# A decoder layer on one core: the same instructions put in order by another of the scheduler's estimates

## The chip, the core and the metric

The kernel runs on one core of one Trainium2 chip. A core has a matrix engine (TensorE, PE in the rows below, with its weight loads as PEld), three elementwise engines (VectorE or DVE, ScalarE or ACT, GpSimd or POOL), an engine that here only issues transfers (SyncE, SP), 16 DMA engines, and two on-chip memories, SBUF for operands and PSUM for the sums of the matmuls. Each engine works off its own list of instructions and waits for the others through semaphores. The metric is the device time of one execution in microseconds, here of one core.

## What is computed

One layer of a decoder for 256 tokens of width 2048, in float32. The reference, cut to its steps:

```python
mod = silu(c) @ w_ada + b_ada                        # shift, scale, gate for both halves
sh1, sc1, g1, sh2, sc2, g2 = split(mod, 6)
h = rmsnorm(x, norm1_g) * (1 + sc1) + sh1
proj = h @ w_in                                      # 2048 x 4928
hq, hf, hi, hg, q_a, kv_a, k_pe = split(proj)
o_a = rmsnorm(hgrn2_chunked(hq, hf, hi, lb)) * silu(hg)         # 8 heads, chunks of 64
qh = rmsnorm(q_a) @ w_q_up ; kv = rmsnorm(kv_a) @ w_kv_up       # latent attention, 8 heads
o_b = rmsnorm(causal_attention(qh, kh, v))                      # blocks of 128 queries
x = x + g1 * (concat(o_a, o_b) @ w_out)
h2 = rmsnorm(x, norm2_g) * (1 + sc2) + sh2
x = x + g2 * moe(h2)        # best of 4 groups, best 2 of its 8 experts, 32 experts in all
```

All weights are read from memory once, 572 MB, of which 403 MB are the 32 experts' matrices.

## The kernel before

The weights come as a stream of chunks, most of them 2 MB (128 partitions by 4096), in a fixed list `items`. `ring_fill` (L163) issues the loads on SP as slots come free: four slots in the first part, two more from the output projection on (L830), one more before the experts (L868). `ring_done` (L181) returns a slot. The list is consumed in order by a loop that calls one function for each kind of chunk.

The first part holds everything ahead of the experts. `ad1_chunk` (L243) and `adt_chunk` (L264) make the shift and scale of the first norm; the first takes its chunks through TensorE (L252), the second, for twelve chunks that lie transposed in memory, through VectorE with two passes over 2048 columns each (L271, results named `adt`), which are given the scheduler's `high_priority(-120)`. `ada_chunk` (L283) makes g1, sh2, sc2 and g2 out of eight chunks each, with eight matmuls per chunk onto one row (L293, `pada`); its end for g1 and g2 is four additions on one partition (L302). `dense` (L410) is every projection: each 512-column tile of the weights is split into a high and a low part by ScalarE (L417) and VectorE (L418), both written to a tile named `split` of which there are four, and six matmuls (L425 to L427 or L432 to L434, accumulator `pacc`) use it. The input projection's partial sums are added in SBUF by VectorE (L457, `proj`). `mla` (L707) is the latent attention of four heads, called twice: scores `psc` (L786, L788), mask, maximum and exponential (L791 to L797), transposes `ppT` (L802) and their copy `pT` (L804), the product with v `pov` (L810), division (L814, `o`), norm over each head (L477 to L479, L195 to L202), multiplication (L818) and transposes `pmt` (L824). `hgrn` (L483) is the recurrence of four heads, also called twice: gates (L490 to L498, with a sigmoid L491 and a logarithm L497 on ScalarE), scan (L501), exponentials and products (L503 to L515), transposes `ptr` (L520), `pA`, `ua`, `ub`, `uc`, `po`. Then follow the output projection with the residual (`w_out`) and the router.

In the second part, 32 experts of six chunks each pass by: gate and up matmuls (L1040, `pgu`), down matmuls (L1016, `py`), gathering the tokens (L970) and adding the outputs (L993).

What stands where in the lists of the engines is decided when the program is built. The framework (`tile.TileContext`) takes the instructions as the code emits them, keeps the dependencies between tiles, and orders them by priority and by an estimate of when each can start. In the kernel before the estimate is a simple one. The list of loads, SPREAD, EARLY and the buffer counts are written by hand and are the same in both.

## Time and profile before

| | us |
|---|---|
| median of 3 runs | 1505.64 (1505.19 to 1507.08) |
| profiled execution | 1505.27 |
| its span | 1503.0 |
| TensorE busy | 1127.9 (75%) |
| VectorE busy | 588.6 (39%) |
| ScalarE busy | 338.4 (23%) |
| mean transfer rate | 383 GB/s |

The span is the time from the first to the last event of the profile; the execution's own time has 2.3 us around it. The shares are means over two parts that differ, so the page is read by slices and windows first, then by what each engine waited for in a window. A busy TensorE is not one at its peak: its matmuls overlap, so where a count matters the distance from one matmul's start to the next is used.

### The profile page before, as it was taken

The numbers are of one execution on the slowest core, as the hardware profiler recorded it, in microseconds if no ns is written. First come the engines' busy times: TensorE is split into PE (matmuls) and PEld (weight loads), VectorE is DVE, ScalarE is ACT, GpSimd is POOL, SyncE is SP. The second block draws the span as 40 slices with busy tenths as digits, with TensorE's granted clock in tenths as the row PEclk, the third lists the DMA queues.
The fourth block names the chain that finished last, engine by engine and source line by source line (L and its number), as shares of the span: only waits on it lengthen the run. The fifth ranks groups of instructions, "written<-read, shape, count | busy, mean of one in ns | idle before, by whom it ended". The sixth has DMA issues, their size and how long they took to land.

```text
span 1503.0 us, 22846 instructions
## 1 busy us (share of the span) xinstructions
PE 1127.9 (75%) x9893; PEld 687.8 (46%) x9893; DVE 588.6 (39%) x1200; ACT 338.4 (23%) x699; POOL 5.0 (0%) x9
## 2 busy tenths in 40 slices
PE   5989999979999989675666666657657756666556
PEld 2868887737568756333323323323423423332222
DVE  4699998769765552220120121113112112112112
ACT  5634446536435423000100100100100100000000
POOL 0000000000000000000000000000000000000000
PEclk7999999989999999888888888879888889779787
DMA  9788796877979798999999999999999999999995
GB/s 373 263 332 356 298 352 257 315 302 313 369 293 376 293 373 343 430 429 430 430 430 430 430 430 429 429 431 430 430 430 430 430 431 430 430 429 429 431 430 222
DMA packets 44143, 575.61 MB, mean 383 GB/s; under 512 B 4858, under 2 KB 5114, under 8 KB 8712
## 3 DMA queue, kind: packets, MB, share of 16 engines
q1 hardware_dynamic: 42496, 570.56, 91.4%
q10 hardware_dynamic: 1544, 3.56, 0.6%
q8 instruction: 79, 1.29, 0.3%
q14 instruction: 24, 0.20, 0.0%
HBM read 572.00 MB, written 2.11 MB: 382 GB/s over the span
## 4 chain that ended last, share of the span: by engine, by line
DMA 51%; PE 37%; DVE 9%; ACT 1%; issue 1%; SPq 0%; ACTq 0%; DVEq 0%
DMA wch<-in_w_gu_dram 37%; DMA wch<-in_w_down_dram 13%; PE pgu L1040 5%; PE pacc L433 5%; PE pacc L434 5%; PE pacc L432 5%; PE pada L293 3%; PE py L1016 3%; PE pcmb L993 2%; PE pgat L970 2%; DVE wch L271 2%; DVE split L418 2%; DVE proj L457 1%; PE pacc L427 1%; PE pacc L425 1%; PE pacc L426 1%
## 5 line engine op out<-in xcount | busy, mean ns | idle before, releaser
L1040 PE MATMUL pgu<-wch,XT 128*32 128x256 f32 x4096 | 309.7, 455 | 201.0 <-DMA wch<-in_w_gu_dram 201.0
L1040 PEld LDWEIGHTS pgu<-wch,XT 128*32 128x32 f32 x4096 | 139.2, 126 | 361.0 <-DMA wch<-in_w_gu_dram 253.9
L1016 PE MATMUL py<-wch,hT 128*32 128x256 f32 x2048 | 167.9, 485 | 76.8 <-DMA wch<-in_w_down_dram 72.1
L1020 DVE TENSOR_TENSOR Y<-py,gate 32x256 f32<-32x256 f32 x256 | 107.6, 420 | 216.5 <-PE py L1016 213.6
L1005 DVE TENSOR_TENSOR hid<-sgu,pgu 128x128 f32<-128x128 f32 x32 | 9.2, 287 | 462.2 <-ACT sgu L1003 462.2
L418 DVE TENSOR_TENSOR split<-wch,split 128x512 fp32r<-128x512 f32 (+2 forms) x248 | 159.5, 666 | 69.6 <-ACT split L417 69.0
L417 ACT ACTIVATE split<-wch 128x512 fp32r<-128x512 f32 (+2 forms) x248 | 148.0, 614 | 161.2 <-PE pacc L434 98.4
L1016 PEld LDWEIGHTS py<-wch,hT 128*32 128x32 f32 x2048 | 78.9, 133 | 155.0 <-issue 60.8
L1003 ACT ACTIVATE sgu<-pgu 128x128 f32<-128x128 f32 x32 | 8.9, 277 | 602.5 <-PE pgu L1040 602.5
L975 ACT ACTIVATE XT<-pgat,sh,a 128x128 f32<-128x128 f32 x128 | 48.1, 456 | 223.1 <-PE pgat L970 223.0
L433 PE MATMUL pacc<-split,hhi 128*128 128x512 f32 (+1 forms) x192 | 75.5, 393 | 7.0 <-DVE split L418 7.0
L425 PE MATMUL pacc<-hhi,split 128*128 128x256 f32 x256 | 72.4, 286 | 2.8 <-ACT hhi L388 2.2
L426 PE MATMUL pacc<-hlo,split 128*128 128x256 f32 x256 | 72.7, 285 | 1.7 <-DVE hlo L389 1.7
L434 PE MATMUL pacc<-split,hlo 128*128 128x512 f32 (+1 forms) x192 | 73.7, 386 | 0.0
L432 PE MATMUL pacc<-split,hhi 128*128 128x512 f32 (+1 forms) x192 | 72.9, 392 | 0.8 <-DVE proj L457 0.7
L427 PE MATMUL pacc<-hhi,split 128*128 128x256 f32 x256 | 72.2, 285 | 1.1 <-DVE split L418 1.1
L293 PE MATMUL pada<-wch,ca 128*1 128x512 f32 x512 | 68.7, 602 | 3.3 <-DVE pada L288 3.3
L993 PE MATMUL pcmb<-Y,pwt 128*128 128x512 f32 x128 | 59.2, 605 | 15.5 <-DVE Y L1020 15.5
L970 PEld LDWEIGHTS pgat<-ohr,x 128*128 128x128 f32 x512 | 63.4, 205 | 10.7 <-issue 9.8
L970 PE MATMUL pgat<-ohr,x 128*128 128x128 f32 x512 | 66.8, 291 | 0.7 <-DVE sm L937 0.7
L271 DVE SCALAR_TENSOR_TENSOR wch<-wch,gate 128x2048 f32<-128x2048 f32 x24 | 54.8, 2284 | 0.0
L457 DVE TENSOR_TENSOR proj<-proj,pacc 128x512 f32<-128x512 f32 (+1 forms) x80 | 51.2, 662 | 0.8 <-PE pacc L434 0.4
(311 smaller groups left out, 1215.4 us busy)
## 6 DMA issues: line engine op xcount, KB each, us to landing
wch<-in_w_gu_dram SPq DMA_DIRECT2D x128, 2048.0 KB, 31.1
wch<-in_w_down_dram SPq DMA_DIRECT2D x64, 2048.0 KB, 31.5
wch<-in_w_ada_dram SPq DMA_DIRECT2D x36, 2048.0 KB, 10.1
wch<-in_w_ada_t_dram SPq DMA_DIRECT2D x12, 2048.0 KB, 7.9
wch<-in_w_in_dram SPq DMA_DIRECT2D x12, 2048.0 KB, 9.2
wch<-in_w_out_dram SPq DMA_DIRECT2D x8, 2048.0 KB, 9.5
wch<-in_w_in_h_dram SPq DMA_DIRECT2D x8, 1024.0 KB, 8.9
wch<-in_w_in_dram SPq DMA_DIRECT2D x3, 1664.0 KB, 7.0
```

Source lines behind the costliest of these rows:

```text
L293: PE.matmul(acc[b][32 * j:32 * j + 1, :], ca[:, kt:kt + 1], w[:, o:o + 512], start=kt == 0, stop=kt == 15)
L417: S.activation(s[:, 0, :ncol], w, AF.Copy)
L418: V.tensor_sub(s[:, 1, :ncol], w, s[:, 0, :ncol])
L426: PE.matmul(o, s[:, 0, c], lo, start=False, stop=False, skip_group_check=True)
L432: PE.matmul(o, hi[:, c], s[:, 0, :ncol], start=first, stop=False)
L433: PE.matmul(o, hi[:, c], s[:, 1, :ncol], start=False, stop=False)
L434: PE.matmul(o, lo[:, c], s[:, 0, :ncol], start=False, stop=stop)
L970: PE.matmul(ps[:, 128 * i:128 * i + 128], x2[kt // 4][:, t, 128 * (kt % 4):128 * (kt % 4) + 128], ohr[:, t], start=t == 0, stop=t == 1)
L993: PE.matmul(ps, PWT[G4][:, 128 * t:128 * t + 128], Y4[j // 2][:, 512 * (j % 2):512 * (j % 2) + 512], start=True, stop=True)
L1016: PE.matmul(py[32 * j:32 * j + 32, :256], H["T"][:, 32 * kt:32 * kt + 32], w[:, 1024 * kt + 256 * j:1024 * kt + 256 * j + 256], start=kt = ...
L1020: V.tensor_mul(Y[q][r:r + 32, 256 * j:256 * j + 256], py[32 * j:32 * j + 32, :256], gate[32 * j:32 * j + 32, c:c + 256])
L1040: PE.matmul(gu[32 * j:32 * j + 32, :256], XT[G4][kt // 8][:, kt % 8, 32 * e4:32 * e4 + 32], w[:, 1024 * i + 256 * j:1024 * i + 256 * j + 2 ...
```

## The change

```diff
-    with tile.TileContext(nc) as tc:
+    with tile.TileContext(nc, schedule_with_timeline_sim=True) as tc:
```

The scheduler now orders the instructions by a simulation of the engines' timelines. The instructions and their tiles are the same, but for one table load more on ScalarE. In the lists of the engines 2,276 lines of TensorE differ, 943 of VectorE, 481 of ScalarE and 48 of SP, none of GpSimd.

SP at the start of the program (`x` the four pieces of the input, `cst` the constants, `wch` a chunk of weights), before and now in one piece:

```order
 L93 DMA pos_i<-in_pos_dram 128x2
-L172 DMA wch_97<-in_w_ada_dram 128x4096
 L212 DMA x_89<-in_x_dram 128x2x512
 L212 DMA x_90<-in_x_dram 128x2x512
 L212 DMA x_91<-in_x_dram 128x2x512
 L212 DMA x_92<-in_x_dram 128x2x512
+L172 DMA wch_97<-in_w_ada_dram 128x4096
 L217 DMA cst<-in_cst_dram 128x1120
 L172 DMA wch_102<-in_w_ada_dram 128x4096
```

The first chunk of weights has moved behind the four pieces of x.

VectorE at one of the transposed chunks (`wch_258`) in the second quarter of the input projection, before:

```order
L271 SCALAR_TENSOR_TENSOR wch_258_1585,adt_291_1822<-wch_258_1585,gate_84 128x2048
L457 TENSOR_TENSOR proj_66_383<-proj_66_383,pacc_278_1716 128x512
L457 TENSOR_TENSOR proj_66_383<-proj_66_383,pacc_279_1717 128x512
L418 TENSOR_TENSOR split_288_1800<-wch_256_1580,split_288_1800 128x512
L418 TENSOR_TENSOR split_289_1809<-wch_256_1580,split_289_1809 128x512
L280 TENSOR_TENSOR a1_132<-adt_291_1822,pc_79 128x1
L418 TENSOR_TENSOR split_295_1832<-wch_271_1694,split_295_1832 128x512
L281 SCALAR_TENSOR_TENSOR a1_132<-a1_132,pc_79 128x1
L418 TENSOR_TENSOR split_296_1841<-wch_271_1694,split_296_1841 128x512
L418 TENSOR_TENSOR split_297_1850<-wch_271_1694,split_297_1850 128x512
L457 TENSOR_TENSOR proj_71_406<-proj_71_406,pacc_284_1780 128x512
L457 TENSOR_TENSOR proj_71_406<-proj_71_406,pacc_285_1781 128x512
```

and now:

```order
L418 TENSOR_TENSOR split_261_1592<-wch_228_1379,split_261_1592 128x512
L418 TENSOR_TENSOR split_262_1601<-wch_228_1379,split_262_1601 128x512
L418 TENSOR_TENSOR split_263_1610<-wch_228_1379,split_263_1610 128x512
L457 TENSOR_TENSOR proj_47_274<-proj_47_274,pacc_250_1540 128x512
L457 TENSOR_TENSOR proj_47_274<-proj_47_274,pacc_251_1541 128x512
L271 SCALAR_TENSOR_TENSOR wch_258_1585,adt_291_1822<-wch_258_1585,gate_84 128x2048 x2
L418 TENSOR_TENSOR split_264_1619<-wch_228_1379,split_264_1619 128x512
L418 TENSOR_TENSOR split_267_1632<-wch_228_1379,split_267_1632 128x512
L418 TENSOR_TENSOR split_268_1647<-wch_228_1379,split_268_1647 128x512
L277 TENSOR_TENSOR sh1_131<-adt_291_1822,pc_79 128x1
L418 TENSOR_TENSOR split_269_1662<-wch_228_1379,split_269_1662 128x512
L280 TENSOR_TENSOR a1_132<-adt_291_1822,pc_79 128x1
```

The chunk's two passes, which had thirteen instructions between them, are now one behind the other (x2), and stand eleven splits earlier.

TensorE at the end of the second call of `mla`, before, where the last product `pov` lies 47 rows ahead of `pmt`:

```order
L427 MATMUL pacc_622_3604<-hhi_274_1704,split_626_3650 128x256
L293 MATMUL pada_612_3541<-wch_609_3530,ca_109 1x512 x8
L293 MATMUL pada_612_3541<-wch_613_3551,ca_109 1x512 x5
L824 MATMUL pmt_592_3382<-cst_78,o_565_3272 128x128 x4
L824 MATMUL pmt_593_3389<-cst_78,o_565_3272 128x128 x4
L312 MATMUL pcol_610_3533<-cst_78,rows_130 128x128 x4
```

and now:

```order
L788 MATMUL psc_579_3332<-kpT_558_3231,qz_363_2208 128x128
L802 MATMUL ppT_582_3348<-cst_78,s_580_3341 128x128 x4
L810 MATMUL pov_578_3327<-v_519_3051,pT_583_3353 128x128 x4
L824 MATMUL pmt_592_3382<-cst_78,o_565_3272 128x128 x4
L824 MATMUL pmt_593_3389<-cst_78,o_565_3272 128x128 x4
L312 MATMUL pcol_610_3533<-cst_78,rows_130 128x128 x4
L432 MATMUL pacc_664_3864<-split_670_3902,mhi_590_3380 128x512
```

The tiles of the input projection and the modulation chunks that stood between the scores, the product and `pmt` now stand ahead of the scores.

VectorE at the same place, before, from the division of the last product on:

```order
L814 TENSOR_TENSOR o_565_3272<-pov_578_3327,den_566_3273 128x512
L478 TENSOR_REDUCE sm_584_3362<-sq_585_3363 128x4
L418 TENSOR_TENSOR split_625_3635<-wch_608_3520,split_625_3635 128x512
L418 TENSOR_TENSOR split_626_3650<-wch_608_3520,split_626_3650 128x512
L515 TENSOR_TENSOR proj_71_406<-proj_71_406,sg_629_3671 128x1024
L478 TENSOR_REDUCE sm_584_3362<-sq_586_3366 128x4
L498 TENSOR_SCALAR proj_66_383<-proj_66_383 128x1024
L479 TENSOR_SCALAR sm_584_3362<-sm_584_3362 128x8
```

and now, from the copy ahead of it:

```order
L804 COPY pT_583_3353<-ppT_582_3348 128x512
L515 TENSOR_TENSOR proj_71_406<-proj_71_406,sg_629_3671 128x1024
L498 TENSOR_SCALAR proj_66_383<-proj_66_383 128x1024
L501 SCALAR_TENSOR_TENSOR b_630_3679<-cst_78,d1_631_3680 128x256
L814 TENSOR_TENSOR o_565_3272<-pov_578_3327,den_566_3273 128x512
L501 SCALAR_TENSOR_TENSOR b_630_3679<-cst_78,d1_631_3680 128x256 x3
L478 TENSOR_REDUCE sm_584_3362<-sq_585_3363 128x4
L478 TENSOR_REDUCE sm_584_3362<-sq_586_3366 128x4
L503 TENSOR_TENSOR d1_631_3680<-b_630_3679 128x1024
L504 TENSOR_TENSOR d3_632_3681<-b_630_3679 128x1024
L479 TENSOR_SCALAR sm_584_3362<-sm_584_3362 128x8
L511 TENSOR_TENSOR kn_633_3682<-kn_633_3682,proj_66_383 128x1024
```

The recurrence's scan, exponentials and products (L501 to L513) now stand ahead of the attention's norm, L818 is the seventh instruction behind the last row shown, and ScalarE has the sigmoid and the logarithm of the recurrence (L491, L497) and its four exponentials (L505 to L508) ahead of or among the steps of that norm.

## Rows read from the trace of the kernel before

**Rows 1.** Page, busy tenths of 40 slices of the span (9 is 90% or more).

```profile
PE   5989999979999989675666666657657756666556
...
DVE  4699998769765552220120121113112112112112
...
DMA  9788796877979798999999999999999999999995
```

**Rows 2.** Page, chain that ended last, shares of the span by engine.

```profile
DMA 51%; PE 37%; DVE 9%; ACT 1%; issue 1%; SPq 0%; ACTq 0%; DVEq 0%
```

**Rows 3.** Windows: stretch, length, busy us (instructions) by engine, PEclk, DMA share, GB/s.

```profile
0.00:60.00 60.00, 44.25 (x225) 27.26 (x226) 27.50 (x80) 34.93 (x64) 1.16 (x5) 0.86 0.82 314
60.00:214.00 154.00, 143.56 (x873) 123.08 (x872) 148.03 (x238) 69.50 (x121) 0.00 (x0) 0.99 0.86 330
...
354.00:432.00 78.00, 71.72 (x515) 47.51 (x513) 59.37 (x125) 37.34 (x69) 2.86 (x3) 0.98 0.77 307
...
573.00:1476.00 903.00, 589.74 (x6663) 297.93 (x6655) 162.86 (x370) 63.60 (x184) 0.00 (x0) 0.85 1.00 429
```

**Rows 4.** Timeline of PE, 469 to 473 us: start, us, engine, line, operation.

```profile
469.38 0.40 PE L432 MATMUL pacc<-split,mhi 128*128 128x512 f32 x1
...
470.78 0.40 PE L432 MATMUL pacc<-split,mhi 128*128 128x512 f32 x1
```

**Rows 5.** Waits of PE, 0 to 60 us: total, times, longest.

```profile
PE pad L252 <- DMA wch<-in_w_ada_dram: 9.9, 2, 9.6
```

**Rows 6.** Waits of SP, 0 to 60 us.

```profile
SPq L217 <- DMA wch<-in_w_ada_dram: 4.9, 1, 4.9
```

**Rows 7.** Timeline of DVE, 136 to 152 us (x4: four in a row).

```profile
136.08 2.28 DVE L271 SCALAR_TENSOR_TENSOR wch<-wch,gate 128x2048 f32<-128x2048 f32 x1
...
145.09 2.49 DVE L418 TENSOR_TENSOR split<-wch,split 128x512 fp32r<-128x512 f32 x4
```

**Rows 8.** DMA issues, 153.5 to 154.5 us: KB each, median us to landing.

```profile
wch<-in_w_ada_t_dram SPq DMA_DIRECT2D x1, 2048.0 KB, 7.8
```

**Rows 9.** Waits of PE, 214 to 241 us.

```profile
PE pqa L667 <- DVE proj L663: 2.5, 1, 2.5
```

**Rows 10.** Waits of PE, 241 to 340 us.

```profile
PE pmt L824 <- DVE o L818: 4.6, 1, 4.6
PE pada L293 <- DVE pada L288: 3.3, 1, 3.3
```

**Rows 11.** Line 302 in 300 to 312 us: duration ns min/median/max, first and last start.

```profile
L302 DVE TENSOR_TENSOR brows<-brows,pada x4: 667/682/694, 305.9 to 310.3; 1x512 f32<-1x512 f32 x4
```

**Rows 12.** Timeline of PE, 271 to 281 us.

```profile
272.53 0.39 PE L788 MATMUL psc<-kpT,qz 128*128 128x128 f32 x2
...
277.24 0.44 PE L802 MATMUL ppT<-cst,s 128*128 128x128 f32 x2
```

**Rows 13.** Timeline of ACT, 387 to 400 us.

```profile
394.45 1.28 ACT L491 ACT_TABLE_LOAD   x1
395.74 1.06 ACT L491 ACTIVATE sg<-proj 128x1024 f32<-128x1024 f32 x1
...
397.86 1.28 ACT L189 ACT_TABLE_LOAD   x1
```

**Rows 14.** Waits of PE, 340 to 461 us.

```profile
PE ptr L520 <- DVE d L513: 5.1, 1, 5.1
```

**Rows 15.** Groups of DVE by line, 390 to 425 us: busy us, mean ns of one.

```profile
L501 DVE TENSOR_TENSOR_SCAN b<-cst,d 128x256 f32<-128x256 f32 x4 | 2.7, 681 | 0.0
...
L503 DVE TENSOR_TENSOR d<-b 128x1024 f32<-128x1024 f32 x1 | 1.2, 1224 | 0.0
...
L818 DVE TENSOR_TENSOR o<-o,sm 128x1024 f32<-128x1024 f32 x1 | 1.2, 1197 | 0.0
```

**Rows 16.** Timeline of DVE, 565 to 568 us.

```profile
566.45 0.14 DVE L940 CAST rounds<-sm 1x1 int32<-1x1 f32 x1
```

**Rows 17.** Timeline of SP, 570 to 600 us.

```profile
573.41 8.02 SPq L172 DMA_DIRECT2D wch<-in_w_gu_dram  x3
```

## The prediction

> **What bounds the kernel now.** I read the view by slices first. From the 17th slice on (601 us) the transfers fill every slice and TensorE is half to three quarters busy [rows 1]; the chain that ended last is DMA for half of the span [rows 2]. The windows say the same: 573 to 1476 has a DMA share of 1.00 at 429 GB/s, while before 573 the share is 0.77 to 0.86 and TensorE or VectorE is full [rows 3]. So the program is two parts put end to end. The expert stream needs its 903 us whatever the order of the engines, as long as seven chunks lie ready when it starts; its order of instructions hardly moves. Only the first part, up to the first expert chunk consumed at 573 us, can gain or lose, and what it gains or loses goes one to one into the total. I therefore sum the shift of that point. The profiled execution took 1505.27 us (span 1503.0, 2.3 outside), 0.4 under the median of 1505.64, so the sum is made against 1505.3.
>
> In the first part the work is the same before and after: the same matmuls, the same elementwise instructions. What counts is how long TensorE stands. One 512-column tile of a projection occupies it for 1.40 us from first matmul to first matmul [rows 4]. All its matmuls up to 573 us, counted so, add up to about 477 us (matmul start to matmul start, over the timeline); about 78 us of the first 560 it stands, of which 22 in the first 60 us and some 17 in 60 to 214, where VectorE has 148 of 154 us busy and sets the pace [rows 3]. I go through the places where it stands, and ask what stands there in the new order.
>
> **Start: -4 us.** The first matmuls with a weight wait 9.9 us for two chunks of the shift and scale weights [rows 5]. In front of the second sits the load of the constants, which SP held back 4.9 us for the landing of the first chunk [rows 6]: in the built program the two share a completion counter. In the new order x goes out first and the constants share a counter with a small load, so the constants and all weight loads behind them leave up to 4.9 us earlier. x, 2 MB, now lands ahead of the first chunk, which needs it to wait but little: that part can't be worth more than 4.9, and I take 4 (2 to 6).
>
> **The VectorE stretch, 60 to 214 us: +8 us.** Here each of the eleven later transposed chunks costs VectorE two passes of 2.28 us, 2.21 each when the next instruction is at hand [rows 7]. Before, they stand apart, with four to ten split and add instructions between them; VectorE makes a split in 0.60 us [rows 7] and TensorE uses it up in 1.40, so one pass of 2.21 is covered by the three or four splits that lie ready. Now both stand together, 4.42 us. I follow two cycles. VectorE makes three splits, does two adds on a finished accumulator and goes into the pair; the splits behind wait for its end. TensorE has used up its stock and stands 4.0 us in the first cycle; in the next the adds themselves must wait 1.5 us for matmuls that were held up, the pair ends later, and TensorE stands 2.2 us; in a third it is 2.8. Eleven times the mean of 3.0 is 33 us, against 17 before: +16. VectorE's own total up to the end of this stretch is 1 us smaller than before, so by its work alone nothing is lost but the waits for loads below: +4. Worked forward from the last pair but one (VectorE has 9 us more work behind it there, 149 instead of 140, and 4 of waits for loads; TensorE has 3 less before it up to 214) I get +10. In this stretch too each transposed chunk is loaded into the slot that the one before it has just left: 7.4 to 9.3 us of VectorE's work between release and use, where a 2 MB load alone needs 7.8 from issue to landing [rows 8], and another 4.9 when one is ahead of it; six such loads give 0.5 to 2.7 us each, 6 to 7 in all, half of it inside the stands already counted. I take +8 between the ends 3 and 16.
>
> By the Trainium skill ("DMA: Bandwidth & Descriptors", section "Anatomy of one DMA", given there for the gpsimd path; SP issues the loads here), a transfer costs about 2.0 us plus its bytes over 436 GB/s, which for 2 MB is an estimate of 6.8 us. By that figure the 7.4 us would cover each load and the term would be some 3 us smaller; the trace has 7.8 for it [rows 8], a microsecond more, and the trace decides.
>
> **Before latent attention, 214 to 241 us: +2 us.** TensorE waits 2.5 us for the normalised low-rank query [rows 9], after one modulation chunk of eight matmuls (1.83 us) that filled the rest of that gap. The new order has used that chunk earlier, in between tiles; the gap is open to its full 4.3.
>
> **First attention and recurrence, 241 to 354 us: +5 us.** Three stands are listed now: 4.6 for the head-normalised output, 3.3 for the clearing of the accumulator of the next modulation row [rows 10], the rest are short; counted from matmul to matmul the stretch loses 13. All three vanish: the up-projection of the second four heads now lies where they were. In their place: (a) four additions of 0.65 us on one partition [rows 11] now precede the copy that the second product waits for: 4 x 0.65 + 0.6 = 3.2; (b) twice the copy itself, uncovered, 1.1, and (c) a softmax chain of 4.7 us from the scores to their transposes [rows 12] with one chunk of 1.83 under it, 2.9; (d) the up-projection's first split stands on VectorE behind the recurrence's first steps, which need ScalarE's sigmoid and logarithm with a table load of 1.28 us ahead of each [rows 13]: about 8; (e) 3 at the transposes and products of the recurrence. Together 18, less 13. Between -2 (if (d) is what VectorE alone needs, 4.7, and (e) nothing) and +9.
>
> **Second attention and recurrence, 354 to 461 us: +11 us.** The stand for the recurrence's transposes, 5.1 us [rows 14], goes. But the tiles that stood behind the last product are now consumed before it. Then TensorE has nothing between the scores of the last block and their transposes (4.7 us as above, 0.2 of it work: +4.5), nothing while the copy is made (+0.9), and nothing between the product and the transposes of the head-normalised output. For those VectorE has to come through, by the rows of its forms [rows 15], each less the 0.08 by which neighbours overlap, one multiplication of o 0.6, three scans 1.8, two reductions 0.6 each, five passes of L503's shape 1.14 each, five small ones 0.4 and L818 1.1 us: 10.8. Ahead of it stand L515 and a scan that need ScalarE: table load 1.28, sigmoid 1.0, table load, then the logarithm, of the sigmoid's shape, 1.0 [rows 13], so that the multiplication starts 6.2 us after the transposes of the scores although the product is ready at 2.5; and ScalarE has four passes of 1.0 us before the small logarithm and exponential of the norm, which adds 1.3. L818 ends at 18.3, TensorE goes on at 18.5: it stands 16. With 1.4 at the first split of the output projection the new stands are 22.8; the old stretch loses 11, counted alike. So +11.7, taken as +11; if ScalarE were never late it would be 12 instead of 16 and the term +7, and it can't exceed +14 by the same rows.
>
> **The rest: 0.** In the output projection (461 to 550 us) TensorE's tiles follow each other in both orders; modulation chunks slip in between. In the router's tail the four additions of L302 come ahead of the last logits and no longer in between the steps after them: 3 us later and 3 us shorter. SP reads the number of extra rounds before one of the first expert loads; the value is there at 566.5 [rows 16] and that load has to wait for its slot until 573.4 anyway [rows 17].
>
> Sum: -4 + 8 + 2 + 5 + 11 = +22, so 1505.3 + 22 = 1527 us.
>
> **The rivals.** *The stands close, and the kernel is faster.* The old stands at 4.6, 3.3 and 5.1 us and the start vanish, and the new ones lie under work that I put at the wrong side. The point it hangs on is the end of the second attention: if L818 ends within 2 us of the product, that stretch wins 9 instead of losing 11, and with the VectorE stretch at its low end the time is 1505.3 - 4 + 3 + 2 - 2 - 9 = 1495. For it speaks that TensorE has chunks to take in; against it that TensorE takes them in the order in which they stand, and none stands there. Chance 0.13.
>
> *It evens out.* The pairs cost only VectorE's waits for loads (+3), the first recurrence is even, the second costs +4 because ScalarE is ahead: -4 + 3 + 2 + 0 + 4 = +5 at most, and a slightly better start brings it to 1502.6 to 1508.6, which is the 0.2% that a measurement of this kernel can't tell from no change. That the switch moves nothing is excluded by the order, which differs in 2,276 lines on TensorE. Chance 0.08.
>
> *The loads fall behind.* If the single slot's loads queue behind others each time (12 instead of 8 us), the VectorE stretch costs +16, and the loads of the first recurrence, released 8 to 10 us of work before use, cost some 8 more: 1505.3 + 22 + 8 + 8 = 1543 and above. Chance 0.05.
>
> **How the numbers follow.** The forecast (1509 to 1543) has 0.74, the three rivals 0.13, 0.08 and 0.05. Faster 0.13, same 0.08, slower 0.79. The ends of the terms added one way give 1505.3 - 6 + 3 + 0 - 2 + 7 = 1507, and the other way 1505.3 - 2 + 16 + 2 + 9 + 14 = 1544, which would take all at once; so as to leave out no more than two in ten the range goes down to 1502 and up to 1546.
>
> **What would show it.** The first chunk of the experts is consumed at about 595 instead of 573 us, with 903 us behind it as now. The waits view shows TensorE waiting once, for some 15 us, for L818 at the end of the second attention, and for none of 5.1 at L520. VectorE's two passes of 2.28 us follow each other, and in 60 to 214 us TensorE's busy time falls while the first matmuls with a weight start some 4 us earlier. I would be wrong if the waits at L824 are short, or if the windows show the stretch up to 214 us no longer than now.

## The result: 59 us slower

| | before | after |
|---|---|---|
| median, us | 1505.90 (1505.19 to 1507.08, 4 runs) | 1565.18 (1562.86 to 1567.33, 4 runs) |
| profiled span, us | 1503.0 | 1564.3 |
| first matmul of the first expert chunk (L1040) at, us | 571.4 | 631.3 |

The ratio is 1.0391 (95% interval 1.0378 to 1.0403), 59 us, where 22 were forecast; the time lies above the range of 1502 to 1546. The last line of the table says where: the first expert chunk is consumed 59.9 us later, and from there on the two kernels run alike. The mean granted clock of the whole span is the same (0.888 and 0.887). So the frame of the forecast held (only the first part counts, and it counts one to one), and the size of its terms did not.

The page of the changed kernel, busy share in 40 slices and the chain that ended last by engine and line, to be held against [rows 1, 2]:

```profile
PE   6979898979959998967666666657666666667555
DMA  9697866887763967799999999999999999999995
DMA 54%; PE 36%; DVE 6%; ACT 2%; issue 2%; SPq 0%; ACTq 0%; DVEq 0%
DMA wch<-in_w_gu_dram 38%; DMA wch<-in_w_down_dram 12%; PE pada L293 5%; PE pacc L433 5%; PE pgu L1040 4%; PE pacc L432 4%; PE pacc L434 4%; DMA wch<-in_w_ada_t_dram 2%; PE py L1016 2%; DVE wch L271 2%; PE pcmb L993 2%; DMA wch<-in_w_ada_dram 1%; PE pacc L426 1%; PE pacc L427 1%; PE pacc L425 1%
```

One entry in the chain I had given no price at all: `pada` L293, the modulation chunks, 5% here and 3% in the chain of the kernel before. Windows of the changed kernel (length, busy time of each engine with its instructions, clock, DMA share, rate), against [rows 3]:

```profile
60.00:214.00 154.00, 135.33 (x791) 115.50 (x790) 139.65 (x223) 65.79 (x113) 0.00 (x0) 0.96 0.80 314
470.00:640.00 170.00, 161.50 (x848) 106.96 (x851) 83.49 (x189) 61.18 (x122) 1.91 (x2) 0.95 0.64 248
632.00:1535.00 903.00, 589.02 (x6679) 298.03 (x6671) 162.98 (x370) 64.45 (x186) 0.00 (x0) 0.85 1.00 428
```

The 903 us of the stream are as full as before. In 60 to 214 us both TensorE and VectorE do less than before: the engine that I had called the one that sets the pace has itself lost 8 us. In 470 to 640 us TensorE looks well used, 161.5 of 170 us, and yet the stretch takes longer; that is for the most part not waiting, but matmuls that cost more. What TensorE waits for in the changed kernel, 0 to 640 us (total, times, longest):

```profile
PE pmt L824 <- DVE o L818: 14.5, 1, 14.5
PE pad L252 <- DMA wch<-in_w_ada_dram: 9.9, 3, 7.0
PE pacc L433 <- DVE split L418: 7.3, 6, 2.2
PE pacc L426 <- DVE hlo L389: 7.2, 3, 4.5
PE prank L926 <- DVE sel L921: 5.4, 1, 5.4
PE pov L810 <- DVE pT L804: 4.9, 3, 3.0
PE pqa L667 <- DVE proj L663: 4.4, 1, 4.4
...
PE pacc L432 <- ACT split L417: 3.5, 1, 3.5
PE ptr L520 <- DVE d L513: 3.4, 1, 3.4
```

To lay the loss out by stretches although the orders differ, I took the start of the same matmul in both traces and subtracted TensorE's work up to it, each matmul at its usual distance to the next (0.233 us for L432 to L434, 0.117 for L425 to L427, and 0.23 for L293, as the prediction had it). What remains is time in which TensorE stood or went slower than its usual pace; the clock is in it too. Ahead of the first expert chunk the granted clock was at the lower of its two levels, 1.2 instead of 2.4 GHz, for 75 us instead of 48, and TensorE was busy for 52 of these instead of 29. Groups of eight that take 1.1 to 1.2 us took some 2.0 at that level (last section), so by an estimate from these rows some 10 of the 59 us are work at the lower clock. The table gives the increase of that time over the kernel before, in us, and the same for two of the experiments below (chunks whole alone, and chunks whole and passes apart, which is the last run below and also has the last piece of x moved forward):

| up to (us in before) | predicted | after | chunks whole | apart and whole |
|---|---|---|---|---|
| start, to 72 | -4 | +1.0 | +2.6 | 0.0 |
| VectorE stretch, to 214 | +8 | +11.4 | +8.8 | -2.7 |
| to the low-rank query, 239 | +2 | +3.5 | +0.6 | +1.0 |
| first attention and recurrence, to 395 | +5 | +9.0 | +3.8 | +2.8 |
| second, to 467 | +11 | +18.8 | +16.1 | +14.5 |
| output projection and router, to 571 | 0 | +16.1 | +10.0 | +2.0 |
| sum | 22 | 59.8 | 41.9 | 17.6 |

The ends of the third, fourth and fifth stretch are single tiles, and the orders have done different work around them, so a few us between neighbours are not to be trusted; the sums are. For example, if the two attentions are divided at the first transposes of the first recurrence's output (L563, 344.7 us in before) and no longer at 395, the changed kernel loses some 11 and 17 us in them and the last column has some 7 and 10.

### The profile page after: what moved, and what is told of

Read it like the earlier page. It is cut to its first block, busy times and chain, and to the rows that moved or that the text cites. A ratio compares the mean times of both kernels' runs of the same rounds, so it can differ in the third digit from the quotient of the medians.

```text
span 1564.3 us, 22859 instructions
## 1 busy us (share of the span) xinstructions
PE 1158.7 (74%) x9893; PEld 695.9 (44%) x9893; DVE 590.9 (38%) x1200; ACT 340.2 (22%) x700; POOL 5.0 (0%) x9
## 4 chain that ended last, share of the span: by engine, by line
DMA 54%; PE 36%; DVE 6%; ACT 2%; issue 2%; SPq 0%; ACTq 0%; DVEq 0%
DMA wch<-in_w_gu_dram 38%; DMA wch<-in_w_down_dram 12%; PE pada L293 5%; PE pacc L433 5%; PE pgu L1040 4%; PE pacc L432 4%; PE pacc L434 4%; DMA wch<-in_w_ada_t_dram 2%; PE py L1016 2%; DVE wch L271 2%; PE pcmb L993 2%; DMA wch<-in_w_ada_dram 1%; PE pacc L426 1%; PE pacc L427 1%; PE pacc L425 1%
## 5 line engine op out<-in xcount | busy, mean ns | idle before, releaser
L1040 PE MATMUL pgu<-wch,XT 128*32 128x256 f32 x4096 | 309.6, 454 | 200.5 <-DMA wch<-in_w_gu_dram 200.3
L1040 PEld LDWEIGHTS pgu<-wch,XT 128*32 128x32 f32 x4096 | 139.7, 126 | 359.0 <-DMA wch<-in_w_gu_dram 249.7
L1016 PE MATMUL py<-wch,hT 128*32 128x256 f32 x2048 | 164.2, 475 | 84.0 <-DMA wch<-in_w_down_dram 79.9
L293 PE MATMUL pada<-wch,ca 128*1 128x512 f32 x512 | 86.4, 613 | 0.0
L433 PE MATMUL pacc<-split,hhi 128*128 128x512 f32 (+1 forms) x192 | 75.6, 395 | 4.4 <-DVE split L418 4.4
L434 PE MATMUL pacc<-split,hlo 128*128 128x512 f32 (+1 forms) x192 | 73.6, 387 | 0.2 <-DVE hlo L389 0.2
L425 PE MATMUL pacc<-hhi,split 128*128 128x256 f32 x256 | 71.5, 286 | 0.0
L427 PE MATMUL pacc<-hhi,split 128*128 128x256 f32 x256 | 69.3, 287 | 2.7 <-DVE split L418 2.7
L970 PEld LDWEIGHTS pgat<-ohr,x 128*128 128x128 f32 x512 | 64.7, 206 | 13.7 <-issue 12.9
L970 PE MATMUL pgat<-ohr,x 128*128 128x128 f32 x512 | 69.8, 295 | 0.5 <-DVE ohr L960 0.5
L432 PE MATMUL pacc<-split,hhi 128*128 128x512 f32 (+1 forms) x192 | 63.0, 393 | 4.4 <-DVE proj L457 4.4
L426 PEld LDWEIGHTS pacc<-hlo,split 128*128 128x128 f32 x256 | 49.4, 193 | 8.4 <-DVE hlo L389 7.9
```

The source lines that it names most:

```text
L293: PE.matmul(acc[b][32 * j:32 * j + 1, :], ca[:, kt:kt + 1], w[:, o:o + 512], start=kt == 0, stop=kt == 15)
L426: PE.matmul(o, s[:, 0, c], lo, start=False, stop=False, skip_group_check=True)
L432: PE.matmul(o, hi[:, c], s[:, 0, :ncol], start=first, stop=False)
L433: PE.matmul(o, hi[:, c], s[:, 1, :ncol], start=False, stop=False)
L434: PE.matmul(o, lo[:, c], s[:, 0, :ncol], start=False, stop=stop)
L970: PE.matmul(ps[:, 128 * i:128 * i + 128], x2[kt // 4][:, t, 128 * (kt % 4):128 * (kt % 4) + 128], ohr[:, t], start=t == 0, stop=t == 1)
```

## A cause that the forecast did not have: modulation chunks in pieces

TensorE in the changed kernel in the output projection (start, us, engine, line, operation; the trace has two records for each matmul of L293):

```profile
517.95 1.03 PE L293 MATMUL pada<-wch,ca 128*1 128x512 f32 x6
518.91 0.73 PE L432 MATMUL pacc<-split,mhi 128*128 128x512 f32 x2
519.57 1.03 PE L293 MATMUL pada<-wch,ca 128*1 128x512 f32 x4
520.53 0.50 PE L433 MATMUL pacc<-split,mhi 128*128 128x512 f32 x1
```

Three matmuls of a chunk take 0.96 us from their start to the next instruction, two take 0.96 as well. A whole chunk of eight takes 1.83. The trace of the kernel before had it all along, where chunks are cut in the output projection and in the router's tail:

```profile
529.37 1.89 PE L293 MATMUL pada<-wch,ca 128*1 128x512 f32 x14
531.19 0.50 PE L432 MATMUL pacc<-split,mhi 128*128 128x512 f32 x1
...
548.95 1.02 PE L293 MATMUL pada<-wch,ca 128*1 128x512 f32 x2
549.90 1.09 PE L632 MATMUL px2T<-cst,x 128*128 128x128 f32 x8
550.92 1.04 PE L293 MATMUL pada<-wch,ca 128*1 128x512 f32 x8
551.89 2.05 PE L640 MATMUL plog<-wr,x2T 128*128 128x128 f32 x16
```

One matmul takes 0.95 us to the next instruction, four take 0.97, seven 1.82. So my 0.23 per matmul was a mean over whole chunks, and no price of one matmul. Each further piece can cost up to 0.95 us more. In the list of the kernel before the 256 matmuls of L293 stand in 32 runs, in that of the changed kernel in 54, of which 31 have four or fewer (11 in the kernel before); each of these 31 occupies TensorE for 0.95 to 0.96 us in the trace. L293 is busy 86.4 us where it was 68.7.

By the Trainium skill ("TensorE: Matmul & The Clock Gate", section "Part 3: Packing small matmuls — row/col tiling") small matmuls that address different strips of the array run side by side, so that a pack lasts about as long as one of its members. The code fits that (L293 writes row 32j, with j from 0 to 3), and the rows agree: one, three or four last the same.

```diff
-                PE.matmul(acc[b][32 * j:32 * j + 1, :], ca[:, kt:kt + 1], w[:, o:o + 512], start=kt == 0, stop=kt == 15)
+                with tc.high_priority(400 if k or j else 0): PE.matmul(acc[b][32 * j:32 * j + 1, :], ca[:, kt:kt + 1], w[:, o:o + 512], start=kt == 0, stop=kt == 15)
```

**Chunks whole, in the changed kernel.**

> The changed kernel, with the seven later matmuls of a modulation chunk (L293) given a high priority, so that a chunk's eight stay together: 31 runs of them in TensorE's list where the changed kernel has 54 and the kernel before 32. Theory of the broken chunks: in the changed kernel's timeline a run of one to four of these matmuls takes about 0.95 us up to the next instruction, one of eight 1.83, so each chunk that is cut costs again; L293 is busy 86.4 us there against 68.7 before. Counted by runs of up to four, this order has 67 against 87, some 20 us less of TensorE, of which I expect 10 to 18 in the time: 1547 to 1555, with L293 busy for 66 to 69 us and most of the gain between 470 and 640 us. Theory that only TensorE's stands count (wait for the normalised heads 14.5 us, wait for splits): those stay, the matmuls fill gaps anyway, and the time stays at 1563 to 1567.

Measured: 1546.96 us (1.0269, 1.0254 to 1.0284), 18.2 us less than the changed kernel. Its group of L293:

```profile
L293 PE MATMUL pada<-wch,ca 128*1 128x512 f32 x512 | 63.6, 596 | 2.2 <-DMA wch<-in_w_ada_dram 2.2
```

22.8 us less of busy time, and 18.2 us in the time, while the wait at L824 is still 13.9. The theory that only waits count is out. The place is not the one that I had expected: by the table 6 us of the gain lie in the output projection and the router, and the rest ahead of them. In the router's tail a part is eaten up by a load that comes late in this order (below).

**The same edit in the kernel before.**

> The kernel before, with the seven later matmuls of a modulation chunk (L293) given a high priority: 21 runs in TensorE's list instead of 32, by runs of up to four 64 instead of 72. Theory of the broken chunks: some 9 us less of TensorE, at least half of it on the path: 1496 to 1501, with L293 busy for 60 to 64 us instead of 68.7. Rival: these chunks lie in gaps where TensorE waits anyway, and a chunk in one piece delays what it stood between: 1503 to 1508.

Measured: 1500.04 us (0.9964, 0.9951 to 0.9977): faster than both kernels, L293 busy for 60.2 us. 5.6 of the 8.5 us are in the time.

**Chunks broken, in the kernel before** (the same line with `-40 * (4 * k + j)` as the priority).

> The kernel before, with each later matmul of a modulation chunk (L293) 40 steps lower in priority than the one ahead of it: 41 runs instead of 32, by runs of up to four 80 instead of 72, and the rest of TensorE's list moved only around them. Theory of the broken chunks: about 9 us more of L293's busy time (76 to 79 us instead of 68.7), and 5 to 9 us in the time: 1511 to 1515. Rival (the pieces fill gaps and cost nothing): 1503 to 1508.

Measured: 1518.05 us (1.0077, 1.0064 to 1.0090), 12.4 us more, and

```profile
L293 PE MATMUL pada<-wch,ca 128*1 128x512 f32 x512 | 78.4, 603 | 6.9 <-DVE pada L288 4.2
```

The busy time is as expected (9.7 us more), and L293 also waited 3.6 us longer, for the clearing of its accumulator and for a load. But the 12.4 us are not the price of the pieces alone. The first expert's first matmul starts only 0.1 us later than before (571.55); the last seven modulation matmuls, with the broadcast of g2 (L949) that needs them, have slid in among the first experts' work:

```profile
586.04 1.02 PE L293 MATMUL pada<-wch,ca 128*1 128x512 f32 x4
...
592.91 5.40 PE L1016 MATMUL py<-wch,hT 128*32 128x256 f32 x64 [0.45 <-ACT hT L1009]
```

The first down product starts 8.2 us later (584.69 before), and from the third expert on the whole stream is some 14 us late. No run here separates pieces from late chunks in this order; the prices to go by are those of the runs with whole chunks and of the next one.

**Held together by fours** (the same line with `400 if j else -60 * k`).

> The kernel before, with the matmuls of a modulation chunk (L293) held together by fours, the four of one half of the chunk at high priority, the second four 60 steps lower: 32 runs in TensorE's list as in the kernel before, but all of 4, 8, 12, 16 or 20, so that by groups of up to four there are 64 instead of 72. Theory that up to four such matmuls cost as much as one (0.95 us): 4 to 8 us less than before, about as the whole chunks gave (5.6), 1498 to 1502. Theory that every change from other matmuls to these and back costs, whatever stands in the run: as many runs as before, 1504 to 1508.

Measured: 1502.71 us (0.9977, 0.9968 to 0.9986), L293 busy for 62.7 us. As many runs as before, and 6.0 us less of busy time: it is the fours that count, and the changes between kinds of matmul cost little beside them (0.97 us for four in one run and 1.83 for eight leave some 0.1 per run). In the time 3.2 us came of it, a little less than I had expected, and the intervals of this kernel and of the one with whole chunks overlap.

## Pairs of passes on VectorE

**Passes apart, in the changed kernel.** Each pass k of a transposed chunk was ordered behind a split of its own; the dependency carries no wait, it only tells the scheduler what stands first.

```diff
-                V.scalar_tensor_tensor(wk, wk, 1.0, gate, op0=OP.mult, op1=OP.mult, accum_out=r[:, k:k + 1])
+                p = V.scalar_tensor_tensor(wk, wk, 1.0, gate, op0=OP.mult, op1=OP.mult, accum_out=r[:, k:k + 1]); after_split(p, -5 + 4 * k)
```

> The changed kernel, with each of the 24 passes over a transposed chunk (L271) put behind a split of its own, four splits from one pass to the next: no pair is left. Theory of the pairs and just-in-time loads: the part of 12 us that the changed kernel has lost by 214 us goes for the most part, 4 to 10 us less, so 1555 to 1561; the waits of TensorE for L389 (7.2 us in 60 to 250 us), for L457 (4.4) and of VectorE for a transposed chunk's load (6.4 in four) fall to under half. Rival: the passes only bring other work late (the split behind each pass, the chunk's slot is free later and the next load follows later), VectorE is as full as before, and the time is 1562 to 1568.

Measured: 1542.6 us (1.0246, 1.0231 to 1.0261), 22.6 us less, more than the theory of the pairs had allowed. By 239 us the whole loss of that part, 15.9 us, is gone. The other 6 to 7 come later and are not the passes': the order moved elsewhere too, L293 is busy 81.5 instead of 86.4 us, and the wait at L824 is 9.6 instead of 14.5. As a price of the pairs this run is not clean, so the next does it the other way round.

**Pairs, in the kernel before.**

```diff
-            with tc.high_priority(-120):
-                V.scalar_tensor_tensor(wk, wk, 1.0, gate, op0=OP.mult, op1=OP.mult, accum_out=r[:, k:k + 1])
+            with tc.high_priority(400):
+                p = V.scalar_tensor_tensor(wk, wk, 1.0, gate, op0=OP.mult, op1=OP.mult, accum_out=r[:, k:k + 1]); after_split(p, -1)
```

> The kernel before, with both passes over a transposed chunk (L271) put behind the same split, the last one that the code has emitted ahead of them, and given a high priority: twelve pairs and no single pass in VectorE's list, the list of loads unchanged. Theory of the pairs (two passes in a row, 4.4 us, outlast the splits that lie ready, whatever else the order does): TensorE stands 8 to 16 us more by 240 us, so 1513 to 1522, since taking the pairs out of the changed kernel gave 16 us up to there. Rival (it was the late loads of the changed order that cost, a pair by itself is made good in the next cycle): 1503 to 1509, and the waits of VectorE for these chunks' loads under 2 us.

Measured: 1520.37 us (1.0098, 1.0082 to 1.0113), 14 us more; by 239 us TensorE has stood 14.6 us longer, and nothing is added behind. Waits in 60 to 241 us, of TensorE and of VectorE:

```profile
PE pacc L433 <- DVE split L418: 11.4, 9, 2.1
PE pacc L427 <- DVE split L418: 4.3, 2, 2.1
...
DVE split L418 <- ACT split L417: 20.1, 30, 1.3
```

VectorE waits for no load here (in the changed kernel 6.4 us in four waits), and the loss by 239 us is nearly that of the changed kernel (15.9). So it is the pair; that the late loads of the changed order fall into stands that are there anyway is what I conclude from that, no run has them without the pairs. Why the loss is not made good in the next cycle stands in the timelines of this run, VectorE at one pair, then ScalarE and TensorE beside it (the number in brackets is the idle time before an instruction, and what ended it):

```profile
130.29 0.69 DVE L418 TENSOR_TENSOR split<-wch,split 128x512 fp32r<-128x512 f32 x1 [0.70 <-ACT split L417]
...
132.10 0.68 DVE L418 TENSOR_TENSOR split<-wch,split 128x512 fp32r<-128x512 f32 x1
132.70 2.28 DVE L271 SCALAR_TENSOR_TENSOR wch<-wch,gate 128x2048 f32<-128x2048 f32 x1
...
134.91 2.28 DVE L271 SCALAR_TENSOR_TENSOR wch<-wch,gate 128x2048 f32<-128x2048 f32 x1
...
137.12 1.27 DVE L457 TENSOR_TENSOR proj<-proj,pacc 128x512 f32<-128x512 f32 x2
...
138.46 0.68 DVE L418 TENSOR_TENSOR split<-wch,split 128x512 fp32r<-128x512 f32 x1
```

```profile
129.63 0.63 ACT L417 ACTIVATE split<-wch 128x512 fp32r<-128x512 f32 x1 [0.77 <-PE pacc L434]
131.03 0.63 ACT L417 ACTIVATE split<-wch 128x512 fp32r<-128x512 f32 x1 [0.77 <-PE pacc L434]
```

```profile
139.20 0.38 PE L427 MATMUL pacc<-hhi,split 128*128 128x256 f32 x1 [2.14 <-DVE split L418]
```

Between pairs VectorE stands too: it waits for ScalarE's half of the split, ScalarE waits for TensorE to give back one of the four split tiles, and that happens once in 1.40 us. VectorE can't work ahead by more than four tiles, whatever time it has. The last split ahead of this pair ends at 132.8 us and the next one at 139.1, because two additions and small instructions stand behind the pair as well; the stock that TensorE had lasted until 137.1, and it stands 2.1 us (1.2 in the mean of the twelve pairs). The time that VectorE spends waiting between pairs is lost. That is how an engine that was busy 148 of 154 us can do 13 us less in the same stretch (135.2 in this run). That the four tiles set the limit is read from these timelines; no run has another number of them.

## The end of the second attention

The last two products and the transposes of the normalised heads in the changed kernel:

```profile
442.80 1.16 PE L810 MATMUL pov<-v,pT 128*128 128x128 f32 x8
...
450.14 2.08 PE L810 MATMUL pov<-v,pT 128*128 128x128 f32 x8 [1.12 <-DVE pT L804]
466.75 1.97 PE L824 MATMUL pmt<-cst,o 128*128 128x128 f32 x8 [14.53 <-DVE o L818]
```

This is the wait that the prediction had put at some 15 us, at its place. TensorE goes on 18.7 us after the transposes of the scores (448.09), where the forecast had 18.5. The stands that it said would go did go: 3.3 us for the cleared accumulator, 4.6 at L824 in the first call [rows 10] and the second recurrence's 5.1 at L520 [rows 14, at 415.7 us] are not in the list above. The 3.4 at L520 in that list stands at 360.1 us, in the first recurrence, where the sum had put 3.

**Four tiles back behind the product.** The first matmul of each group of three in these tiles was ordered behind the last `pov` (`behind`), again without a wait.

```diff
-                    PE.matmul(o, s[:, 0, c], hi, start=first and h % 2 == 0, stop=False, skip_group_check=True)
+                    behind(PE.matmul(o, s[:, 0, c], hi, start=first and h % 2 == 0, stop=False, skip_group_check=True))
```

> The changed kernel, with the four tiles of the last input chunk (splits 623 to 626, L425 to L427) put behind the last product of the second attention (L810): 73 rows of TensorE's list now stand between that product and the transposes of the normalised heads (L824), where the changed kernel has none and the kernel before 47. Theory of the uncovered wait: the 14.5 us at L824 go to under 4 and 10 to 14 us are won, 5 to 7 of the output projection's tiles and the modulation chunks' groups (80 for 87) with them: 1545 to 1555. Rival: the recurrence behind these tiles starts later on VectorE and TensorE waits there for as long: 1560 to 1567.

Measured: 1551.51 us (1.0300, 1.0284 to 1.0316), 13.7 us less, and no wait at L824 any more:

```profile
425.63 1.16 PE L810 MATMUL pov<-v,pT 128*128 128x128 f32 x8 [0.78 <-DVE pT L804]
439.59 1.09 PE L824 MATMUL pmt<-cst,o 128*128 128x128 f32 x8
```

That looked like the term of the sum (11), but part of it is the chunks again: L293 is busy 79.3 instead of 86.4 us here, 7.1 us that may be in the 13.7. And two stands came in at the beginning of this attention, 4.7 us at `ppe` and 2.6 for loads of modulation chunks.

## The start, the tail, and the three repairs at once

**x ahead of the first chunk, in the kernel before** (the first chunk's load and the constants' ordered behind the four of x; TensorE's list is the same).

> The kernel before, with the four pieces of x (L212) ahead of the first chunk of weights (L172) and the constants (L217) behind that chunk in SP's list, as the changed kernel has them; TensorE's list is the same, row for row. Theory of the prediction (the constants no longer wait for the first chunk, everything behind them leaves earlier): 2 to 6 us less, 1500 to 1504. Rival, from the changed kernel's trace, where the first tile with a split of its own came 2.3 us later than before: x now lies in front of the chunk that the first matmuls need, and the time is 1505 to 1509.

Measured: 1506.52 us (1.0001, 0.9992 to 1.0010): no change. SP's timeline in this run (start, us), and TensorE's wait for the first weights in 0 to 60 us, against [rows 5, 6]:

```profile
1.65 2.92 SPq L212 DMA_DIRECT2D x<-in_x_dram  x4
4.62 0.84 SPq L172 DMA_DIRECT2D wch<-in_w_ada_dram  x1
5.50 0.74 SPq L217 DMA_DIRECT2D cst<-in_cst_dram  x1
```

```profile
PE pad L252 <- DMA wch<-in_w_ada_dram: 11.0, 2, 8.2
```

The constants do leave 4.4 us earlier (5.50 against 9.90), as the prediction said. But the first matmul with a weight starts at 17.9 instead of 10.0 us, and the transfers are as busy either way (share 0.75 in the first 12 us and 1.00 at 426 GB/s in the next 18; before, 0.77 and 1.02 at 425). The second group of these matmuls starts at 24.0 instead of 23.0 us: the earlier issue and the x in front of the first chunk come to nothing together. This run changes both, so what either alone is worth stays open. In the changed kernel the first matmul with a weight starts at 17.4 us, where I had expected some 4 us earlier than before.

**Modulation chunks out of the router's tail, in the kernel before** (`3000 if b == "g2" and ch > 4 else 0` as the priority of L293).

> The kernel before, with the last three modulation chunks of g2 (L293) at a high priority, so that one stands earlier between tiles and, of the 25 matmuls that stood in the router's tail behind the last tile, eight are left; the rest of the lists moves only around them. Theory that these matmuls lay under the tail's waits, so that moving them between tiles costs their own time: 17 of them, two chunks of 1.83 us, 3 to 5 us more: 1509 to 1511. Rival (TensorE's time is the same wherever they stand, and the additions of L302 then come earlier, out of the tail's chain): 1502 to 1507.

Measured: 1509.81 us (1.0027, 1.0016 to 1.0038), 3.9 us more. In the changed kernel 11 such matmuls stand behind the last tile, where before there were 24 (the expectation had counted one too many); with whole chunks in the changed kernel there is none. So some 4 us of the last stretch are work that used to lie under the tail's waits. In the profiled execution, 2 us longer than that of before, only 1.1 of it is seen at the gathering (L970); I give the size by the medians alone.

**Three repairs at once** (chunks whole, passes apart, four tiles back), in the changed kernel.

> The changed kernel with three repairs at once: modulation chunks whole (L293, 31 runs), passes over the transposed chunks apart (L271, no pair), and the four last input tiles behind the second attention (L810). Alone the first gave 18.2 us and the second 22.6; the third should give 10 to 14. If the three causes are separate stands and make up the loss of 59 us: 1508 to 1518. If they overlap, so that what one repair frees is lost at the next place: 1520 to 1535.

Measured: 1532.24 us (1.0178, 1.0162 to 1.0194), 33 us less where the single gains add up to 54.5. Part is counted twice: the three had taken 22.8, 4.9 and 7.1 us from L293, but together only 24.0 go (62.4 left), which is 10.8 less. Another part was a new stand that the repairs brought. In this run's timelines, first SP's, then TensorE's:

```profile
561.81 1.89 SPq L172 DMA_DIRECT2D wch<-in_w_gu_dram  x2
563.75 0.55 SPq L589 DMA_DIRECT2D x<-in_x_dram  x1
```

```profile
577.99 2.10 PE L632 MATMUL px2T<-cst,x 128*128 128x128 f32 x8 [4.27 <-DVE x L584]
```

The last piece of x for the residual stands on SP behind expert chunks that wait for a slot, and is issued 0.8 us after the last tile; before, it went out 8.3 us ahead of it.

**The same with that piece first** (all later loads ordered behind it).

> The changed kernel with the three repairs (chunks whole, passes apart, four tiles behind the second attention), and with every load of weights that the code emits later put behind the last piece of x for the residual (L589) in SP's list. With the three repairs alone that piece stood behind expert chunks that wait for a slot, was issued 0.8 us after the last tile of the output projection instead of 8.3 us ahead of it, and the transposes of that piece (L632) came 15.0 us after the last tile instead of 4.7: if that is what ate the sum of the repairs, 8 to 10 us less than 1532, so 1522 to 1525. Rival (the tail is as long for its slower clock and without the modulation chunks that lay in it): 1529 to 1533.

Measured: 1524.02 us (1.0119, 1.0103 to 1.0134), 8.2 us less: the late load was the cause of that stand. This also means that the run with whole chunks alone, where the same load went out 0.8 us after the last tile, would probably have given back more than 18.2 us (TensorE waits 6.6 us at L632 for that piece there).

**And without the four tiles.**

> The changed kernel with chunks whole and passes apart, and the last piece of x for the residual (L589) ahead of the later loads in SP's list; the second attention's end stays as the change left it, without work under its 14 us. If the repairs are separate, 18.2 and 22.6 us and another 8 to 10 for the late piece of x come off: 1514 to 1518, and then the held-back tiles did harm in the combination. If the third repair is worth in the combination what it was alone (13.7), this is slower than the run with all: 1530 to 1538.

Measured: 1525.35 us (1.0133, 1.0117 to 1.0148). Neither theory holds: it is slower than a plain sum, and the third repair is worth 1.3 us here, not 13.7; by the intervals that can't be told from nothing. The waits of TensorE between 235 and 480 us suggest why, first with the four tiles held back, then without:

```profile
PE pov L810 <- DVE pT L804: 5.4, 4, 3.0
PE ppe L769 <- DVE qr L704: 4.7, 1, 4.7
...
PE pada L293 <- DMA wch<-in_w_ada_dram: 3.4, 2, 2.7
```

```profile
PE pmt L824 <- DVE o L818: 9.6, 1, 9.6
PE pov L810 <- DVE pT L804: 7.9, 4, 3.3
```

The tiles can lie at the end of the second attention or at its beginning, and the end that is left bare waits: 9.6 us at L824 in the one, 4.7 at `ppe` and 3.4 for loads in the other. Pieces and pairs gone, the changed kernel is still 19.5 us above the kernel before, and by the table above 17.3 of these lie in the two attentions together, 10 to 14.5 in the second according to where they are divided. That remainder I have located, and not taken away.

## The prediction, step by step

**The frame** was right: the stream is unmoved, the shift of the first expert chunk is the loss. Slower was right, by the places named; the sum was 37 us short.

**Modulation chunks, priced at nothing: the largest miss.** "Modulation chunks slip in between" stood for 0 under "The rest", and each matmul of L293 was counted at 0.23 us everywhere. Whole chunks gave back 18.2 us in the changed kernel and 5.6 in the kernel before; breaking them there cost 12.4 together with the late chunks that this brought. The rows for it (0.95 us for one, 0.97 for four) were in the trace that I had; I had read a mean.

**The VectorE stretch, +8: the right mechanism, half the size.** The pairs cost 14 us in the kernel before, and taking them out of the changed one gave 16 by 239 us. My walk through the cycles had said +16. The step that failed is the next one, where I took VectorE's sum of work as a bound ("by its work alone nothing is lost") and went to the middle. A sum bounds an engine only if it can work ahead, and VectorE can't by more than four tiles. The term for loads was right in size (6.4 us of waits in four, forecast 6 to 7 in six) and wrong in effect: the pairs cost as much without them. The upper end of the term, 16, held. By the Trainium skill ("DMA: Bandwidth & Descriptors", section "Anatomy of one DMA") a chunk was estimated at 6.8 us; the transposed chunks took 7.9 us in the middle from issue to landing in the kernel before and 9.2 in the changed one, so the trace was the better guide, and still nothing hung on it.

**The start, -4: failed.** The wait of SP [rows 6] went as said, and the new order of the first loads was worth nothing as a whole (1506.52 against 1506.39). The step that failed is that x ahead of the first chunk would cost little: the first matmul with a weight starts 7 to 8 us later for it. I had priced a wait of the issuing engine without asking whether the transfers had room.

**The low-rank query, +2:** the wait is 4.4 us instead of 2.5 [rows 9], as forecast (4.3), the stretch +3.5.

**The attentions, +5 and +11:** the changed kernel loses 9.0 and 18.8 there. Without pieces and pairs it loses 17.3 in both, where 16 were forecast, so that the sum of the two terms was near; how near each was depends on where they are divided (2.8 and 14.5 in the table, some 7 and 10 by L563). In the first, two pieces came out as forecast (3.0 us at the product for 3.2, 3.4 at the recurrence for 3) and one smaller (3.5 and 2.2 at the first splits of the up-projection for about 8), so part of the agreement there is luck. The wait for L818 was 14.5 us instead of 16, with the very passes in front of it that the sum had listed.

**The rest, 0: failed,** 16.1 in the changed kernel. In 470 to 640 us the trace has 64 matmuls of L293 in 23 runs that take 26.4 us, where before 56 in 7 runs take 15.3: 11 us. Some 4 are the tail without its chunks; I had looked there only at the four additions of L302. No term of the sum had the lower clock behind a stand either, some 10 us by the estimate above, spread over the rows of the table.

**The rivals.** None came true. Nearest in time was the one on late loads (1543 and above), but the waits for loads are no longer than in the forecast; the right side of the range was passed for another reason. The range had the ends of the terms that were in the sum, and so could not hold a term that was not.

## What to carry to other kernels

Before a sum is made by counts, look for the shortest run of each kind of instruction in the trace, and not only at the mean: a group that shares its cost (here four matmuls for the price of one) loses it as soon as an order cuts it. An engine's sum of work is a bound only as far as its buffers let it work ahead; where a producer has four tiles of stock, a stretch of other work on it costs what exceeds the stock, each time. And repairs that each win alone need not add up: they free the same piece twice, or move a load behind a queue that waits.

## What I had not expected of the hardware

One to four matmuls of L293, with one column of weights each and 512 columns of data, cost TensorE 0.95 to 0.97 us, and eight 1.83. And a stand is paid for again behind it. The granted clock of the changed kernel is 1.00 from 436 to 448 us, 0.50 from 450 to 468 and 1.00 again from 470 to 480. It fell between 448 and 450 us (0.87 there), after TensorE had stood 2.3 us ahead of the last transposes of the scores and before the long stand: the last product already took 2.08 us, where the one before it took 1.16. The eight records of `pmt` then took 1.97 us behind the 14.5 us stand (and again 1.97 behind 9.6 us, in the run without the four tiles), but 1.09 us where TensorE had not stood.
